# A row of maxima for the attention scores: TensorE products and a ScalarE copy replaced by a VectorE transpose and small DMAs

## The chip, the cores and the metric

The kernel runs on one core of a Trainium2 chip. The metric is the time of one execution on the device in microseconds (us). The engines are TensorE (PE, with its weight loads shown apart as PEld), VectorE (DVE), ScalarE (ACT), GpSimd (POOL) and SyncE (SP). Each works through its own list of instructions in order, and waits on semaphores where an operand comes from another engine or from a DMA. A DMA is issued by one of these lists, above all SP's, and lands some time later.

## The reference, cut to what matters

One encoder layer: a normalised input is projected once; eight mLSTM heads and eight attention heads work on the projection; an output projection and a gated feed-forward network follow. The change lies in the attention:

```python
q = rmsnorm(aq.reshape(B, T, A_KV_HEADS, G, HEAD_DIM), q_norm_w)
k = rmsnorm(ak.reshape(B, T, A_KV_HEADS, HEAD_DIM), k_norm_w)
...
s = jnp.einsum('bqhgd,bkhd->bhgqk', qi, k).astype(jnp.float32) * scale
p = jax.nn.softmax(s, axis=-1)
return jnp.einsum('bhgqk,bkhd->bqhgd', p.astype(v.dtype), v)
```

There are 8 query heads and 2 key/value heads of 64 dimensions, one sequence of 2048 tokens and one of 256. All is float32 at the interface.

## The kernel before, in words

The attention is cut into 36 blocks of one head (or of two, for the short sequence) by 512 queries: 32 blocks over 2048 keys and 4 over 256 keys. `attention` (a Python generator) writes the instructions of one block after another, one block ahead of itself:

- `prep` loads the queries of a block (`bq`, SP), transposes them on TensorE into the PSUM tile `pq` (L546) and copies them on ScalarE into two SBUF tiles: `qq` (L549), 128 partitions, the high part of each query in partitions 0 to 63 and the rest (low part) in 64 to 127; and `qm` (L551), the high part alone in partitions 0 to 63. Partition 64 of `qm` is left for the row of maxima. `qq` and `qm` each have two buffers.
- `maxstep` computes scores of 128 queries by 1024 keys in a PSUM tile `px` (L570, two products of 128x512; in the short blocks L564) and VectorE takes their maximum per query into `mx` (L572, L566). Here queries lie on partitions.
- `prep2` reduces the partial maxima to one per query, negated (`m4r`, 128 queries by 4 groups, L578). The scores proper need them the other way round, as a row over 512 queries. Before the change four TensorE products `pr` (L581), of `m4r` broadcast against an identity, do this, and ScalarE copies one partition of the result into partition 64 of `qm` (L583).
- `scores` computes transposed scores, 128 keys by 512 queries, twice per step, into a PSUM tile `ps`: L591 with `qq`, and L592 with `qm` against keys that have a row of ones as row 64, so that the negated maximum is added in the product. ScalarE takes the exponential (L595) and its rounded copy (L596), VectorE the remainder (L597).
- `values` multiplies with the values (L608 to L610), three steps behind the scores; `fin1` and `fin2` divide and store the result for the output projection (`mix_d`).

The PSUM tiles `pq`, `px`, `ps` and, before the change, `pr` share two buffers (tag "sc"). In the loop of a block the max steps of the next block are spread over the first six of its eight steps and `prep2` of the next block follows them.

Around the attention run, on the same engines, the mLSTM heads (their projections are L729, L739 and L757, with inputs `mn`, `mjn`, `mvn` loaded through SP at L726 and L754) and, when these are done, the output projection of phase C (L1009, with loads `cmx` and `cx`, stores `x_d` and `n_d`, all on SP). `run_both` interleaves the generators by fixed costs per step. The final order on each engine is made at build time by the scheduler, which orders the written instructions by priority on a simulated timeline. Removing or adding an instruction therefore moves thousands of others. After both comes the feed-forward network (L1177 and later), where the attention has no part.

Of the kernel before, what the change touches and what calls it, by code (L numbers as in the profile page):

```python
# [9 lines left out]
F32 = mybir.dt.float32  # L10
F32R = mybir.dt.float32r
AF = mybir.ActivationFunctionType
# [5 lines left out]
P = 128  # L18
# [6 lines left out]
HD = 64  # L25
# [60 lines left out]
def f32(ap):  # L86
    return ap.bitcast(F32)
# [380 lines left out]
def attention(g, tc, s1, s2, pp):  # L468


    nc = g.nc
    sp = s1
# [48 lines left out]
    def load_q(n):  # L521

        if n in qzs or n >= len(hbs):
            return
        t = 0
        qz = qzs[n] = sp.tile([P, 4, P], F32R, tag="qz", name=f"bq{n}", bufs=QZB)
        for h, q0, q1 in hbs[n][1]:
            nc.sync.dma_start(f32(qz[:, t:t + q1 - q0]), g.q_d[h, q0:q1].rearrange("n p d -> p n d"))
            t += q1 - q0

    def prep(n):

        s = HB()
        grp, s.qs, k0, k1 = hbs[n]
        s.n = n
        s.last = n == len(hbs) - 1
        load_q(n)
        load_kv(grp, k0, k1)
        s.kv = kv[(grp, k0)]
        s.nq, s.nk = 4, k1 - k0  # L540
        s.N = s.nq * P
        s.nm = "%d_%d" % s.qs[0][0:2]
        qz = qzs.pop(n)
        pq = pp.tile([P, 1024], F32R, tag="sc", name="pq" + s.nm)
        for t in range(s.nq):
            nc.tensor.transpose(pq[:, t * P:(t + 1) * P], qz[:, t, :], g.identr)  # L546
        load_q(n + 1)
        s.qq = sp.tile([P, 512], F32R, tag="qq", name="qq" + s.nm, bufs=2)
        nc.scalar.activation(s.qq[:, 0:s.N], f32(pq[:, 0:s.N]), AF.Copy)  # L549
        s.qm = sp.tile([65, 512], F32R, tag="qm", name="qm" + s.nm, bufs=2)  # L550
        nc.scalar.activation(s.qm[0:HD, 0:s.N], f32(pq[0:HD, 0:s.N]), AF.Copy)  # L551
        s.mx = sp.tile([P, 4, 2], F32, tag="mx", name="mx" + s.nm, bufs=2)
        s.nsp = -(-s.nk * P // 1024)
        s.todo = [(t, z) for z in range(s.nsp) for t in range(s.nq)] if s.nk * P > 512 else [(None, 0)]
        s.steps = len(s.todo)
        return s
# [17 lines left out]
    def prep2(s):  # L574

        nq = s.nq
        m4r = s.m4 = sp.tile([P, 4], F32R, tag="m4r", name="m4r" + s.nm, bufs=2)
        nc.vector.tensor_reduce(m4r[:, 0:nq], s.mx[:, 0:nq, 0:s.nsp], AX.X, ALU.max, negate=True)  # L578
        pr = pp.tile([P, 1024], F32, tag="sc", name="pr" + s.nm)
        for t in range(nq):  # L580
            nc.tensor.matmul(pr[:, t * P:(t + 1) * P], m4r[:, t:t + 1].to_broadcast([P, P]), g.identr, start=True,  # L581
                             stop=True)
        nc.scalar.activation(s.qm[HD:HD + 1, 0:s.N], pr[HD:HD + 1, 0:s.N], AF.Copy)  # L583

    def scores(s, kp):
        kk, kl1 = s.kv[kp // 2][0:2]
# [32 lines left out]
    def fin2(s):  # L619
# [10 lines left out]
        for h, q0, q1 in s.qs:  # L630
# [6 lines left out]
            if h == 5:  # L637
                g.mixed5.update(range(q0, q1))

    cur = prep(0)  # L640
    while cur.todo:
        maxstep(cur)
        yield 0.5
    prep2(cur)
    load_kv(0, 0, NT1, cur.m4)
    pend, fins = [], []
# [8 lines left out]
    for n in range(len(hbs)):  # L655
        nxt = prep(n + 1) if n + 1 < len(hbs) else None
        if n == len(hbs) // 2 - 1:
            load_kv(1, 0, NT1)
        nkp = cur.nk // 2
        for kp in range(nkp):  # L660
            pend.append((cur, *scores(cur, kp)))
            ready = bool(fins)
            if len(pend) > PLAG:
                drain()
            if nxt is not None and nxt.todo:
                for _ in range(-(-len(nxt.todo) // max(nkp - kp - MXE, 1))):
                    maxstep(nxt)
                if not nxt.todo:
                    prep2(nxt)
            if ready:  # L670
                fin2(fins.pop(0))
            yield 2.3
        if nxt is not None and nxt.todo:
            while nxt.todo:
                maxstep(nxt)
            prep2(nxt)
        cur = nxt
# [1002 lines left out]
```

## Time and profile before

| what | value |
|---|---|
| median of 3 runs | 3293.55 us (3292.37 to 3298.3) |
| profiled execution, time | 3297.57 us |
| profiled execution, span | 3295.9 us |
| TensorE busy | 3233.3 us (98%) |
| VectorE busy | 2427.5 us (74%) |
| ScalarE busy | 1959.4 us (59%) |
| mean granted TensorE clock | 0.993 |
| first and last product of the row of maxima (L581) | 217.7 us, 1713.2 us |

The profiled execution lies 4.0 us above the median and within the spread of the runs; 1.7 us of it lie outside the span. Busy times of PE come from matmuls whose ends are modelled and overlap; the distance from one start to the next is what a matmul holds the engine. In the views, "PEq", "SPq" and so on are the instruction lists themselves, with their semaphore and DMA-issuing instructions.

### The profile page before, as it was taken

The numbers are of one execution on the slowest core, as the hardware profiler recorded it, in microseconds if no ns is written. First come the engines' busy times: TensorE is split into PE (matmuls) and PEld (weight loads), VectorE is DVE, ScalarE is ACT, GpSimd is POOL, SyncE is SP. The second block draws the span as 40 slices with busy tenths as digits, with TensorE's granted clock in tenths as the row PEclk, the third lists the DMA queues.
The fourth block names the chain that finished last, engine by engine and source line by source line (L and its number), as shares of the span: only waits on it lengthen the run. The fifth ranks groups of instructions, "written<-read, shape, count | busy, mean of one in ns | idle before, by whom it ended". The sixth has DMA issues, their size and how long they took to land.

```text
span 3295.9 us, 52861 instructions
## 1 busy us (share of the span) xinstructions
PE 3233.3 (98%) x19488; PEld 3016.8 (92%) x19488; DVE 2427.5 (74%) x3683; ACT 1959.4 (59%) x3628; POOL 533.4 (16%) x922
## 2 busy tenths in 40 slices
PE   8999999999999999999999999999999999999998
PEld 7888888888888888878989999999999999999998
DVE  7754676677657777876666999988888788666664
ACT  5645666666665676654453555666676667454543
POOL 4561042213232333200000000000000000010201
PEclk9999999999999999999999999999999999999999
DMA  9973333343345444523327666768576567968663
GB/s 348 319 204 115 114 106 98 100 132 100 103 122 173 136 123 140 155 95 99 111 95 257 236 227 213 247 228 274 203 260 239 194 210 249 320 229 274 217 233 133
DMA packets 358857, 612.27 MB, mean 186 GB/s; under 512 B 31029, under 2 KB 215271, under 8 KB 358599
## 3 DMA queue, kind: packets, MB, share of 16 engines
q1 hardware_dynamic: 328855, 562.09, 50.6%
q0 software_dynamic: 12176, 35.01, 3.9%
q10 hardware_dynamic: 17568, 11.80, 1.1%
q8 instruction: 153, 2.51, 0.3%
q14 instruction: 105, 0.86, 0.1%
HBM read 444.85 MB, written 163.93 MB: 185 GB/s over the span
## 4 chain that ended last, share of the span: by engine, by line
PE 83%; DVE 4%; DMA 4%; issue 4%; ACT 3%; POOL 2%; SPq 1%; ACTq 0%; POOLq 0%; DVEq 0%
PE pa L1177 16%; PE pc L1177 8%; PE pf L1442 7%; PE po L1009 6%; PE pb L1177 4%; PE mj L729 4%; PE mv L739 4%; PE ph L1442 4%; PE pj L248 4%; PE ps L591 3%; PE ps L592 3%; PE pv L610 3%; PE pv L608 3%; PE pv L609 3%; PE px L570 3%
## 5 line engine op out<-in xcount | busy, mean ns | idle before, releaser
L597 DVE TENSOR_TENSOR xx<-pe,xx 128x1024 fp32r<-128x1024 f32 x260 | 318.1, 1224 | 147.7 <-ACT xx L596 145.5
L595 ACT ACTIVATE pe<-ps 128x1024 f32<-128x1024 f32 x260 | 266.2, 1024 | 240.0 <-PE ps L592 217.3
L572 DVE TENSOR_REDUCE mx<-px 128x1 f32<-128x1024 f32 x256 | 310.3, 1217 | 99.8 <-PE px L570 98.2
L596 ACT ACTIVATE xx<-pe 128x1024 fp32r<-128x1024 f32 x260 | 274.9, 1058 | 8.6 <-PE pv L610 3.4
L1395 POOL TENSOR_TENSOR sq<-sq,sq 128x384 f32<-128x384 f32 x38 | 48.4, 1274 | 1380.3 <-ACT sq L1391 1297.7
L1009 PEld LDWEIGHTS po<-cmx,wo 128*128 128x128 f32 x1728 | 228.0, 189 | 18.3 <-DVE cx L1016 1.4
L1009 PE MATMUL po<-cmx,wo 128*128 128x256 f32 x1728 | 235.8, 282 | 1.3 <-DVE cx L1016 1.3
L1182 ACT ACTIVATE u<-pa 128x386 f32<-128x386 f32 (+2 forms) x264 | 128.9, 489 | 169.0 <-PE pa L1177 168.1
L591 PE MATMUL ps<-qq,kk 128*128 128x512 f32 x520 | 213.9, 411 | 5.9 <-DVE mx L572 4.0
L610 PE MATMUL pv<-xx,vv 128*128 128x512 f32 x520 | 210.7, 405 | 3.5 <-DVE xx L597 3.5
L608 PE MATMUL pv<-xx,vv 128*128 128x512 f32 x520 | 209.9, 404 | 2.9 <-ACT xx L596 2.6
L592 PE MATMUL ps<-qm,kl 65*128 65x512 f32 x520 | 209.2, 402 | 0.0
L609 PE MATMUL pv<-xx,vl 128*64 128x512 f32 x520 | 206.8, 398 | 0.0
L729 PEld LDWEIGHTS mj<-mn,wm 128*128 128x128 f32 x1296 | 179.8, 194 | 18.4 <-ACT og L745 4.0
L729 PE MATMUL mj<-mn,wm 128*128 128x256 f32 x1296 | 190.1, 289 | 3.4 <-ACT og L745 3.1
L739 PE MATMUL mv<-wm,mn 128*128 128x256 f32 x1296 | 191.9, 286 | 1.3 <-ACT qb L735 1.3
L739 PEld LDWEIGHTS mv<-wm,mn 128*128 128x128 f32 x1296 | 177.4, 190 | 16.6 <-ACT qb L735 2.3
L248 PE MATMUL pj<-w_a,n1T 128*128 128x512 f32 (+1 forms) x864 | 168.2, 353 | 11.7 <-ACT w_a L105 7.0
L248 PEld LDWEIGHTS pj<-w_a,n1T 128*128 128x128 f32 x864 | 141.5, 192 | 31.5 <-ACT w_a L105 7.0
L570 PE MATMUL px<-kk,qq 128*128 128x512 f32 x512 | 166.3, 405 | 4.0 <-ACT pe L595 2.5
L840 ACT ACTIVATE dm<-dm,tm 128x128 f32<-128x128 f32 x288 | 95.0, 391 | 97.3 <-POOL dm L837 95.2
L1177 PE MATMUL pc<-nt,wb 128*128 128x386 f32 (+2 forms) x792 | 146.2, 338 | 1.3 <-DVE cx L1037 1.3
(332 smaller groups left out, 8073.7 us busy)
## 6 DMA issues: line engine op xcount, KB each, us to landing
mn<-n_d SPq DMA_DIRECT2D x216, 256.0 KB, 3.1
ru<-w_up SPq DMA_DIRECT2D x88, 512.0 KB, 5.0
rs<-wsu_d SPq DMA_DIRECT2D x88, 512.0 KB, 6.2
act_d<-ts SPq DMA_DIRECT2D x33, 768.0 KB, 6.1
nt<-act_d SPq DMA_DIRECT2D x60, 384.0 KB, 4.8
re_t<-wsd_d SPq DMA_DIRECT2D x45, 512.0 KB, 6.1
wsu_d<-tw SPq DMA_DIRECT2D x44, 512.0 KB, 4.5
act_d<-ya SPq DMA_DIRECT2D x99, 192.0 KB, 3.1
```

Of the source, the lines that this page charges most:

```text
L248: nc.tensor.matmul(pjs[t][:, c0:c1], nTs[tiles[t]][:, c, a, :], ws[c][:, b, c0:c1], start=(c == 0 and k == 0), stop=(c == NCC - 1 and k == 2))
L572: nc.vector.tensor_reduce(s.mx[:, t0, z0:z0 + 1], ps, AX.X, ALU.max)
L591: nc.tensor.matmul(o, kk[:, kc:kc + P], s.qq, start=True, stop=False)
L592: nc.tensor.matmul(o, kl1[:, kc:kc + P], s.qm, start=False, stop=True)
L597: nc.vector.tensor_tensor(x[:, 1], pe, f32(x[:, 0]), ALU.subtract)
L608: nc.tensor.matmul(s.pv, vv[:, kt % 4, :], x1, start=kt == 0, stop=False)
L610: nc.tensor.matmul(s.pv, vv[:, kt % 4, :], x2, start=False, stop=kt == s.nk - 1)
L729: nc.tensor.matmul(pj[:, o].rearrange("p (n t) -> p n t", t=P), s.w[c][:, a, o * P:(o + 1) * P], nT[c][:, :, h, :], start=(c + o + k == 0) ...
L739: nc.tensor.matmul(pv[:, o], nT[c][:, o, a, :], s.w[c][:, h, 256:512], start=(c + o + k == 0), stop=(c == NCC - 1 and k == 2 and o == 1))
L1009: nc.tensor.matmul(po[:, o], wo[c][z // 2][:, a, n], mx[c][:, h, :], start=c + o + k == 0, stop=c == NCC - 1 and o == 1 and k == 2)
L1177: m = s.nc.tensor.matmul(p, w[:, aa, c, :], ops[k][:, c, bb, 0:s.n], start=c == 0 and i == 0 and not add, stop=c == NCC // 2 - 1 and i == ...
L1442: nc.tensor.matmul(ps[c], w[:, aa, c, :], t[:, gi - g0, bb, 0:H], start=gi == 0 and m == 0 and not more, stop=gi == NG - 1 and m == 2, ski ...
```

## The change

The copy of the high query rows from PSUM by ScalarE becomes a DMA on SP from `qq` to `qm`, both in SBUF. The four products and ScalarE's copy of one row become: a VectorE transpose in blocks of 32x32, whose input is `m4r` with its four columns repeated eight times, so that within each block of 32 queries the maxima come to lie along a row; and four DMAs on SP that each take four partitions of 32 numbers and put them at the right places of partition 64 of `qm` (16 pieces of 128 bytes in all).

```diff
@@ prep
-        nc.scalar.activation(s.qm[0:HD, 0:s.N], f32(pq[0:HD, 0:s.N]), AF.Copy)
+        nc.sync.dma_start(f32(s.qm[0:HD]), f32(s.qq[0:HD]))
@@ prep2
         nc.vector.tensor_reduce(m4r[:, 0:nq], s.mx[:, 0:nq, 0:s.nsp], AX.X, ALU.max, negate=True)
-        pr = pp.tile([P, 1024], F32, tag="sc", name="pr" + s.nm)
-        for t in range(nq):
-            nc.tensor.matmul(pr[:, t * P:(t + 1) * P], m4r[:, t:t + 1].to_broadcast([P, P]), g.identr, start=True,
-                             stop=True)
-        nc.scalar.activation(s.qm[HD:HD + 1, 0:s.N], pr[HD:HD + 1, 0:s.N], AF.Copy)
+        mt = sp.tile([P, 32], F32, tag="mt4", name="mt" + s.nm, bufs=2)
+        nc.vector.transpose(mt.rearrange("p (r t) -> p r t", t=4), f32(m4r).unsqueeze(1).to_broadcast([P, 8, 4]))
+        for k in range(4):
+            nc.sync.dma_start(f32(s.qm[HD:HD + 1]).rearrange("o (t k i) -> o k t i", t=4, i=32)[:, k],
+                              mt[32 * k:32 * k + 4])
```

The scheduler then puts the instructions of every engine in another order from the first attention block on. First place: TensorE, a block in the middle of the first group (its names end in `_8` with `qq_8_6162`, `qm_8_6164`; the block before it has `_4`). Before, the row's products stand ahead of the scores of the old block's seventh step:

```order
L739 MATMUL mv_5_7097<-wm_6_4824,mn_5_6_7032 128x256 x4
L739 MATMUL mv_5_7097<-wm_7_4825,mn_5_7_7033 128x256 x6
L581 MATMUL pr_8_6547<-identr,m4r_8_6545 128x128 x4
L591 MATMUL ps_4_6_6553<-qq_4_5687,kk_16_12_2584 128x512
L592 MATMUL ps_4_6_6553<-qm_4_5689,kl_16_12_2585 128x512
```

In the changed program nothing of this stands there, and the first scores of the new block read as follows:

```order
L610 MATMUL pv_4_6425<-xx_4_6_6559,vv_16_12_2586 128x512
L591 MATMUL ps_8_0_6775<-qq_8_6162,kk_16_0_2536 128x512
L729 MATMUL mj_5_7042<-mn_5_1_7027,wm_1_4819 128x256 x3
L729 MATMUL mj_5_7042<-mn_5_2_7028,wm_2_4820 128x256
L570 MATMUL px_8_0_0_6791<-kk_16_0_2536,qq_8_6770 128x512
L570 MATMUL px_8_0_0_6791<-kk_16_4_2552,qq_8_6770 128x512
L854 MATMUL mS_15_7386<-qb_7_2397,mkT_7_2396 128x256
L592 MATMUL ps_8_0_6775<-qm_8_6164,kl_16_0_2537 128x512
```

The four products are gone; L591, which needs `qq` alone, now comes seven matmuls ahead of L592, which needs the row, with work of others between the two.

Second place: SP's list at the same block (- is before, + is the change). `mn` are loads of the mLSTM projection, `bq` the queries of the next block, `qm<-mt` the row, `qm<-qq` the high rows of the next block:

```order
 L726 DMA mn_5_4_7030<-n_d 128x512
-L528 DMA bq_6160<-q_d 128x4x128
 L726 DMA mn_5_5_7031<-n_d 128x512
 L726 DMA mn_5_6_7032<-n_d 128x512
 L726 DMA mn_5_7_7033<-n_d 128x512
+L582 DMA qm_8_6164<-mt_8_6547 1x4x32 x4
+L528 DMA bq_6768<-q_d 128x4x128
+L551 DMA qm_8_6772<-qq_8_6770 64x512
 L726 DMA mn_6_0_7408<-n_d 128x512
```

Five DMAs per block are added to SP, the row's four behind the loads of one projection and ahead of the next block's queries, of its high rows, and of the loads of the next projection.

Third place: TensorE where the mLSTM heads end (L893 is their last product) and phase C begins (L1009 is its first). Before:

```order
L893 MATMUL mT_8_16795<-ident,hh_17_16732 128x128
L591 MATMUL ps_8_7_16238<-qq_8_14758,kk_16_12_10418 128x512
L592 MATMUL ps_8_7_16238<-qm_8_14760,kl_16_12_10419 128x512
L591 MATMUL ps_8_7_16238<-qq_8_14758,kk_16_12_10418 128x512
L592 MATMUL ps_8_7_16238<-qm_8_14760,kl_16_12_10419 128x512
L1009 MATMUL po_0_17076<-cmx_0_17008,wo_0_16814 128x256 x3
```

In the changed program:

```order
L609 MATMUL pv_8_17111<-xx_8_5_17209,vl_16_8_10410 64x512
L591 MATMUL ps_8_7_17301<-qq_8_16376,kk_16_12_10418 128x512
L592 MATMUL ps_8_7_17301<-qm_8_16378,kl_16_12_10419 128x512
L591 MATMUL ps_8_7_17301<-qq_8_16376,kk_16_12_10418 128x512
L592 MATMUL ps_8_7_17301<-qm_8_16378,kl_16_12_10419 128x512
L1009 MATMUL po_0_17076<-cmx_0_17008,wo_0_16814 128x256 x3
```

The four `_8` blocks of the second group of heads have the queries `qq_8_14758`, `qq_8_15541`, `qq_8_16376` and `qq_8_16913`. Phase C began with the last scores of the first of them and begins now with the last scores of the third: the attention has moved ahead of the other work by two blocks. The mLSTM's last product stood four rows ahead of phase C and stands 17 rows ahead now, with attention alone between.

## The prediction

> **What bounds the kernel now.** I read the page first, then the busy times by stage, then what TensorE waited for in the stage of the attention.
>
> ```profile
> span 3295.9 us, 52861 instructions
> PE 3233.3 (98%) x19488; PEld 3016.8 (92%) x19488; DVE 2427.5 (74%) x3683; ACT 1959.4 (59%) x3628; POOL 533.4 (16%) x922
> PE 83%; DVE 4%; DMA 4%; issue 4%; ACT 3%; POOL 2%; SPq 1%; ACTq 0%; POOLq 0%; DVEq 0%
> ```
>
> TensorE is busy 98% of the span and holds 83% of the chain that ended last. The attention runs from about 200 to 1760 us. The view by stage (length, then busy us of PE, PEld, DVE, ACT, POOL; at the end granted clock, DMA share, GB/s) shows where it is not the bound:
>
> ```profile
> 200.00:300.00 100.00, 92.72 (x657) 83.79 (x656) 43.86 (x67) 49.62 (x118) 37.57 (x86) 0.98 0.59 166
> 300.00:1380.00 1080.00, 1067.01 (x6694) 933.19 (x6693) 756.31 (x1351) 696.93 (x1543) 300.92 (x589) 0.99 0.40 122
> 1380.00:1450.00 70.00, 60.73 (x298) 44.89 (x297) 58.24 (x103) 48.56 (x86) 6.99 (x12) 0.98 0.37 116
> 1450.00:1750.00 300.00, 300.00 (x1963) 267.38 (x1962) 195.83 (x281) 149.94 (x201) 15.86 (x21) 1.00 0.29 95
> ```
>
> TensorE is idle 7.3 us at the start, 13.0 us in the next 1080, 9.3 us in the 70 us in which the mLSTM heads end and attention is nearly alone (VectorE 83% busy there), and not at all after. So 1380 of these 1550 us are set by how much TensorE has to do. What it waited for, in total us, times and longest, is spread thin:
>
> ```profile
> PE ps L591 <- DVE mx L572: 4.0, 4, 1.7
> PE mj L729 <- ACT og L745: 3.1, 4, 1.0
> PE ps L591 <- ACT qm L583: 0.7, 1, 0.7
> PE mj L729 <- DMA mn<-n_d: 0.3, 1, 0.3
> ```
>
> The row of maxima itself, whose ScalarE copy is L583, cost TensorE 0.7 us of waiting, once. Its price must be looked for in the work.
>
> **The products that go.** Two of the 36 groups of four in the timeline, with what follows each (start, us, count at the end), and the group of all 144 by lines (after the bar: busy us, mean ns, idle before):
>
> ```profile
> 263.61 0.64 PE L581 MATMUL pr<-identr,m4r 128*128 128x128 f32 x4
> 264.08 0.50 PE L546 MATMUL pq<-identr,bq 128*128 128x128 f32 x4
> ...
> 1713.02 0.56 PE L581 MATMUL pr<-identr,m4r 128*128 128x128 f32 x4
> 1713.41 0.45 PE L591 MATMUL ps<-qq,kk 128*128 128x512 f32 x1
> 1713.70 0.39 PE L592 MATMUL ps<-qm,kl 65*128 65x512 f32 x1
> 1713.93 0.40 PE L591 MATMUL ps<-qq,kk 128*128 128x512 f32 x1
> ...
> 1754.73 11.23 PE L1009 MATMUL po<-cmx,wo 128*128 128x256 f32 x93
> ...
> L581 PE MATMUL pr<-identr,m4r 128*128 128x128 f32 x144 | 21.9, 271 | 0.1
> ```
>
> The mean of 271 ns times 144 would be 39 us, but these matmuls overlap. From its start to the next start a group holds TensorE 0.39 us (1713.02 to 1713.41) or 0.47 us (263.61 to 264.08): 36 of them are 14.0 to 16.9 us. The 21.9 us of the group count each tail that overlaps with the next matmul, and are an upper bound. I take 0.43 x 36 = **-15.5 us**.
>
> **ScalarE's copies.** They are 36 x (0.580 + 0.589) = 42 us less, and 43.8 us in which ScalarE stood in its order waiting for the products:
>
> ```profile
> L551 ACT ACTIVATE qm<-pq x36: 575/580/594, 208.7 to 1670.4; 64x512 fp32r<-64x512 f32 x36
> L583 ACT ACTIVATE qm<-pr x36: 572/589/593, 218.6 to 1713.6; 1x512 fp32r<-1x512 f32 x36
> ACT qm L583 <- PE pr L581: 43.8, 20, 5.8
> ```
>
> ScalarE is 65% busy from 300 to 1380 us (696.93 of 1080), so this is no time by itself. It and a PSUM buffer that is now passed on sooner can shorten TensorE's waits on ScalarE and on `mx` (3.1 and 4.0 us in the rows above): 0 to -7 us, taken as **-1**, since these waits have other causes as well.
>
> **More waits on TensorE.** The first L592 of a block waited for one ScalarE semaphore or none, and now for four or five of DMAs. In the order 23 groups of L581 wait for two semaphores, and the trace has 23 instructions on that line that only wait: each semaphore beyond the first costs one.
>
> ```profile
> L581 PEldq EVENT_SEMAPHORE  x23: 51/51/51, 263.0 to 1710.7; - x23
> ```
>
> Counting the waits in both orders, extra ones rise from 452 to 510: 58 x 0.051 = **+3.0 us** if none is covered, 0 if all are.
>
> **The new way of the row.** Reduction, transpose, four issues, landing, and only then L592. VectorE's part, the nearest transposes (64x512), and when the reduction L578 began after the last max product had been given to TensorE, in an early and in the last block:
>
> ```profile
> L578 DVE TENSOR_REDUCE m4r<-mx x36: 143/154/163, 214.7 to 1709.8; 128x4 fp32r<-128x8 f32 x32, 128x4 fp32r<-128x4 f32 x4
> L626 DVE STREAM_TRANSPOSE rs<-rc x36: 698/707/708, 282.9 to 1751.2; 64x512 f32<-64x512 f32 x36
> ...
> 382.48 0.63 PE L570 MATMUL px<-kk,qq 128*128 128x512 f32 x2
> 384.41 0.16 DVE L578 TENSOR_REDUCE m4r<-mx 128x4 fp32r<-128x8 f32 x1
> ...
> 1703.95 0.63 PE L570 MATMUL px<-kk,qq 128*128 128x512 f32 x2
> 1709.79 0.15 DVE L578 TENSOR_REDUCE m4r<-mx 128x4 fp32r<-128x8 f32 x1
> ```
>
> From the end of the products (start plus 0.63) to the reduction are 1.3 and 5.2 us, which are also the least and the most of the 36; the median is 2.3. The transpose has 32 columns instead of 512, so it lies between nothing and 0.7 us; I take 0.15, as for the reduction, which is as small. VectorE gets 36 x 0.15 = 5 us more in 1550, most of it where it waits for others. For issue and landing of SP's DMAs (the list's own time, then from issue to landing; the first pair is `mn`, 128 partitions, the second `mix_d`, the third line has 17 partitions):
>
> ```profile
> L726 SPq DMA_DIRECT2D mn<-n_d x216: 319/320/1403, 167.6 to 979.2; - x108
> DMA to landing us min/median/max: 2.7/3.1/13.0
> L899 SPq DMA_DIRECT2D mix_d<-mmx x9: 319/320/382, 1294.5 to 1423.3; - x9
> DMA to landing us min/median/max: 1.9/2.2/3.4
> L465 SPq DMA_DIRECT2D nm_d<-nst x5: 239/239/791, 214.7 to 235.0; - x5
> ```
>
> Four issues are 4 x 0.239 = 0.96 to 4 x 0.320 = 1.28 us; landing lies between 1.9 and 3.1 us, 2.5 taken for 512 bytes that no row matches. Median chain: 2.3 + 0.15 + 0.15 + 1.1 + 2.5 = 6.2 us; before it was the products and a ScalarE copy, about 1.2 us behind their place. Against it stands the work that the order puts between the last max product and the first L592. For the block of the first place that is 23 matmuls of 512 columns, 30 of 256 and 11 short ones; at 0.23 (1713.70 to 1713.93), 0.12 (11.23/93) and 0.11 us (0.43/4) 10.1 us. Over the 36 blocks it is 6.7 to 13.9 us, median 9.2, and once 30. So the row is about 3 us early at the median. Late reductions (up to 2.9 us over the median) against short covers (2.5 us under it) make a few blocks late: at a landing of 2.5 us some 0.05 us a block on average, at 3.1 us about 0.1. I take **+2 us** for all, 0 to +35 as bounds, the upper one with the rivals.
>
> The Trainium skill (DMA: Bandwidth & Descriptors, "Anatomy of one DMA") gives a fixed cost of about 2.0 us per DMA, most of it the receipt of the write. The trace's shortest 1.9 us agrees. By it the median chain would be 5.7 us and this term +1, an estimate.
>
> SP's list gets 180 DMAs. Behind the row's four stand the next queries, the next high rows and the next projection's `mn`. If the row is late in being given to SP, `mn` is late next. In the order the first `mn` behind the row has 8 us or more of TensorE's work between its buffer coming free and its first use, against 3.1 us of landing; ahead of the row `mn` loads wait for matmuls that end at most 2.9 us after the last max product, before the transpose is due by the median. So I cost the queue at nothing; the high rows (needed some 45 us of work later) too. In phase C the row stands behind stores `x_d` that wait for results of TensorE and VectorE, with 10 to 14 us of cover.
>
> **The order around it.** The attention moves ahead by two blocks (third place). Summing the order at the paces above, the stretch between the last mLSTM projections and an even mixture with phase C holds 39 us of attention in 50 before, 50 in 60 now. Stretch 1380 to 1450 lost 9.3 us for its 39; at the same rate 50 lose 12: **+2.5 us**, between -9 (the new order mends it) and +9 (it is lost twice).
>
> Sum: -15.5 - 1 + 3 + 2 + 2.5 = -9. The profiled execution's 3297.57 would become 3288.5; the median of the runs, 4.0 us lower, 3293.55 becomes **3284.5 us**. This case's own range is -2.5 to -18 us, 3275.5 to 3291.
>
> **The rivals.** *The row comes late (slower).* Place: the first L592 of each block. With a landing of 5.8 us, the longest of `bq`,
>
> ```profile
> DMA to landing us min/median/max: 2.6/3.3/5.8
> ```
>
> which other loads on the queue could cause, the chain is 9.5 us against 9.2; with the spread of both, the mean wait of a block is near 1 us, 35 us in all: -11 + 35 = +24, about 3317 us. It decides from a mean wait of 0.3 us a block (11/36). For it: the scheduler already put L591 and L592 apart, so in its own reckoning the row comes no sooner; and waits cost twice, as the clock shows:
>
> ```profile
> 1005.00:1010.00 5.00, 2.66 (x16) 1.92 (x15) 3.62 (x6) 0.86 (x2) 0.00 (x0) 1.00 0.88 286
> 1010.00:1015.00 5.00, 3.97 (x21) 3.35 (x21) 4.36 (x10) 1.78 (x3) 0.00 (x0) 0.74 0.53 189
> 1015.00:1020.00 5.00, 5.00 (x25) 4.61 (x24) 1.87 (x6) 3.01 (x5) 0.00 (x0) 0.58 0.66 208
> ```
>
> After 3.4 idle us in ten the granted clock is 0.74 and then 0.58, which takes 0.26 x 5 + 0.42 x 5 = 3.4 us more. The Trainium skill (TensorE: Matmul & The Clock Gate, "Part 1: The HAM clock gate") names an idle window of about 3.4 us for the drop to half speed; the trace has the drop with no single gap of that length, so shorter waits are not safe either. Against this rival: the DMA share is 0.29 to 0.40 from 300 us on, and the small `mix_d` land in 2.2 us.
>
> *The work is given back (no change).* The new order loses more where attention is alone, or at the start, where TensorE idles 7.3 us and queries, keys and rows share a DMA system that is 0.59 busy. With the +9 of the alone stretch instead of +2.5 the sum is -2.5: about 3291 us.
>
> *More than the work (faster still).* The freed ScalarE and PSUM buffer remove half of the 29.6 us of TensorE's idling: -9 - 15 = -24, 3269.5 us. For it: 43.8 us of ScalarE's blocked order go. Against: TensorE's rows of waits on ScalarE are small.
>
> **How the numbers follow.** Forecast 0.48, given back 0.22, late 0.20, more 0.10. 0.2% is 6.6 us, about what a measurement of this kernel can tell from no change. The forecast's own range has a quarter of its chance above -6.6. Faster: 0.36 + 0.10 + a little of the second case = 0.50; same: 0.12 + 0.16 = 0.28; slower: 0.20 + 0.02 = 0.22. The range for 8 in 10 leaves out half of the late case and a part of the best: 3268 to 3308 us.
>
> **What would show it.** Right: L581, L551 and L583 on TensorE and ScalarE are gone; rows of `qm` land within 2.5 us or so; L592 has no DMA among what ended its idle time, or a few us in all; TensorE's idling from 200 to 1760 us stays near 30 us, and phase C ends some 10 us sooner. Wrong: "PE ps L592 <- DMA qm" with more than 11 us; a granted clock under 1.00 at block boundaries; `mn` with more than its 0.3 us as a releaser; or a longer stretch with VectorE over 83% busy around 1400 us.

## The result, and the profile after

The changed kernel takes 3276.49 us (median of 6 runs, 3268.71 to 3278.38) against 3293.77 us for the kernel before in the same runs: 0.9934 of it, interval 0.9921 to 0.9948. That is faster by 17.3 us by the medians and by 22 (17 to 26) by the ratio, where the forecast was 9 us. (The ratio stands for a kernel before of about 3297 us, as in the later groups of runs below; the mean of the six runs beside the change is 3294.2 us.) The profiled execution of the change is its fastest one (3268.71 us, 7.8 below its median), and that of before lay 4.0 above its own, so the two traces differ by 28.9 us, more than the kernels do. 5.5 of these lie ahead of the first attention block (its first `pq` is at 202.1 instead of 207.6 us). A difference of a few us between the traces proves nothing, and the sizes below are checked by runs.

The page of the change:

```profile
span 3266.9 us, 52932 instructions
PE 3207.5 (98%) x19344; PEld 2992.7 (92%) x19344; DVE 2437.6 (75%) x3719; ACT 1920.7 (59%) x3556; POOL 538.4 (16%) x922
PE 85%; DMA 4%; issue 3%; DVE 3%; ACT 3%; POOL 2%; SPq 1%; ACTq 0%; POOLq 0%; DVEq 0%
```

144 matmuls fewer, TensorE as full as before. The stages in the same bounds (length, then busy us of PE, PEld, DVE, ACT, POOL; at the end granted clock, DMA share, GB/s):

```profile
200.00:300.00 100.00, 90.51 (x622) 80.53 (x622) 43.36 (x67) 44.28 (x107) 37.42 (x86) 0.97 0.54 156
300.00:1380.00 1080.00, 1073.84 (x6700) 936.15 (x6699) 790.02 (x1390) 690.54 (x1508) 298.03 (x586) 1.00 0.40 125
1380.00:1450.00 70.00, 64.65 (x337) 49.35 (x335) 62.93 (x112) 48.61 (x90) 14.15 (x20) 1.00 0.39 119
1450.00:1750.00 300.00, 294.58 (x2042) 267.99 (x2043) 198.77 (x319) 133.44 (x191) 12.91 (x18) 1.00 0.44 143
```

TensorE idles more at the start (9.5 us instead of 7.3) and after 1450 us (5.4 instead of 0), and less between: 6.2 us instead of 13.0 from 300 to 1380, 5.4 instead of 9.3 in the 70 us after it. The attention itself ends earlier, by far more than its work shrank: the last `pv` starts at 1675.3 us instead of 1749.1, and phase C then runs longer alone. What TensorE waited for from 200 to 1760 us (total us, times, longest):

```profile
PE mj L729 <- DMA mn<-n_d: 4.9, 3, 4.1
PE po L1009 <- DVE cx L1016: 3.9, 2, 2.6
PE pv L610 <- DVE xx L597: 2.6, 6, 0.8
...
PE ps L591 <- DVE mx L572: 1.4, 3, 0.9
...
PE ps L592 <- DMA qm<-mt: 1.0, 1, 1.0
```

The row of maxima was late once in 36 blocks, by 1.0 us. New at the head is `mn`, the load of the mLSTM projection, with 0.3 us before. The instructions that the change adds (count, then shortest, median and longest ns):

```profile
L580 DVE STREAM_TRANSPOSE mt<-m4r x36: 178/211/214, 209.7 to 1614.4; 128x32 f32<-128x32 f32 x36
L582 SPq DMA_DIRECT2D qm<-mt x144: 572/577/699, 210.6 to 1617.0; - x144
L551 SPq DMA_DIRECT2D qm<-qq x36: 502/534/1546, 203.6 to 1570.0; - x36
L592 PEldq EVENT_SEMAPHORE  x73: 51/51/199, 214.4 to 1619.3; - x73
L570 PEldq EVENT_SEMAPHORE  x10: 51/51/1126, 220.1 to 957.4; - x10
```

One of the row's four DMAs holds SP's list for 0.577 us, and one of the high rows for 0.534, where the larger DMAs in the prediction's rows took 0.239 to 0.320.

**Where the time went.** For each trace I took TensorE's matmuls in order of time, from the first `pq` to the end of the last `po`, and split each distance from one start to the next into the idle time that the trace puts ahead of the second one and the rest, which the first one held. This stage is 1595.6 us before and 1570.3 after. The loss of clock is half of the time in which the trace has the clock at half speed and TensorE is not idle.

| part of the stage | before | after | change |
|---|---|---|---|
| products `pr` (L581), start to start | 15.5 | 0 | -15.5 |
| time lost to the granted clock | 8.4 | 1.6 | -6.8 |
| other work of TensorE | 1543.0 | 1543.2 | +0.2 |
| idle: waits for `mx` and for the exponential `pe` | 9.1 | 4.8 | -4.3 |
| idle: waits for `mn` | 0.3 | 4.9 | +4.6 |
| idle: wait for the row | 0.0 | 1.0 | +1.0 |
| idle: all others | 19.3 | 14.7 | -4.6 |

This is one trace of each kernel. Which of these rows belong to the change, and which to this one execution and order, is told by the traces of the experiments below.

### The profile page after: what moved, and what is told of

Its sections match the earlier page's. It is cut to its first block, busy times and chain, and to the rows that moved or that the text cites. A ratio compares the mean times of both kernels' runs of the same rounds, so it can differ in the third digit from the quotient of the medians.

```text
span 3266.9 us, 52932 instructions
## 1 busy us (share of the span) xinstructions
PE 3207.5 (98%) x19344; PEld 2992.7 (92%) x19344; DVE 2437.6 (75%) x3719; ACT 1920.7 (59%) x3556; POOL 538.4 (16%) x922
## 4 chain that ended last, share of the span: by engine, by line
PE 85%; DMA 4%; issue 3%; DVE 3%; ACT 3%; POOL 2%; SPq 1%; ACTq 0%; POOLq 0%; DVEq 0%
PE pa L1177 17%; PE pc L1177 9%; PE pf L1442 7%; PE po L1009 5%; PE ph L1442 4%; PE pb L1177 4%; PE mv L739 4%; PE mj L729 4%; PE pv L610 3%; PE ps L591 3%; PE ps L592 3%; PE pv L608 3%; PE pv L609 3%; PE px L570 3%; PE pj L248 2%
## 5 line engine op out<-in xcount | busy, mean ns | idle before, releaser
L597 DVE TENSOR_TENSOR xx<-pe,xx 128x1024 fp32r<-128x1024 f32 x260 | 319.3, 1229 | 142.4 <-ACT xx L596 139.6
L595 ACT ACTIVATE pe<-ps 128x1024 f32<-128x1024 f32 x260 | 265.2, 1022 | 229.1 <-PE ps L592 204.6
L1009 PEld LDWEIGHTS po<-cmx,wo 128*128 128x128 f32 x1728 | 221.2, 189 | 16.1 <-DVE cx L1016 4.2
L1009 PE MATMUL po<-cmx,wo 128*128 128x256 f32 x1728 | 227.7, 281 | 3.9 <-DVE cx L1016 3.9
L591 PE MATMUL ps<-qq,kk 128*128 128x512 f32 x520 | 211.3, 406 | 3.6 <-DVE mx L572 1.4
L592 PE MATMUL ps<-qm,kl 65*128 65x512 f32 x520 | 208.2, 401 | 1.0 <-DMA qm<-mt 1.0
L729 PEld LDWEIGHTS mj<-mn,wm 128*128 128x128 f32 x1296 | 180.4, 192 | 26.0 <-DMA mn<-n_d 5.8
L729 PE MATMUL mj<-mn,wm 128*128 128x256 f32 x1296 | 192.2, 287 | 7.8 <-DMA mn<-n_d 4.9
L570 PE MATMUL px<-kk,qq 128*128 128x512 f32 x512 | 166.6, 407 | 2.3 <-ACT pe L595 1.6
```

What stands on the lines that cost most here:

```text
L591: nc.tensor.matmul(o, kk[:, kc:kc + P], s.qq, start=True, stop=False)
L592: nc.tensor.matmul(o, kl1[:, kc:kc + P], s.qm, start=False, stop=True)
L597: nc.vector.tensor_tensor(x[:, 1], pe, f32(x[:, 0]), ALU.subtract)
L729: nc.tensor.matmul(pj[:, o].rearrange("p (n t) -> p n t", t=P), s.w[c][:, a, o * P:(o + 1) * P], nT[c][:, :, h, :], start=(c + o + k == 0) ...
L1009: nc.tensor.matmul(po[:, o], wo[c][z // 2][:, a, n], mx[c][:, h, :], start=c + o + k == 0, stop=c == NCC - 1 and o == 1 and k == 2)
```

## The experiments

The theory after the result: the gain is the products' 15.5 us and a few more, because their place was dear too (the first half held, the second did not show in the kernel's own gain, as the traces under "The order alone" tell). A product `pr` takes one of two PSUM buffers (tag "sc") through which every `pq`, `px` and `ps` must pass, and holds it until the maxima are there. The rivals: the relief of ScalarE (two copies less a block); the order that the scheduler happened to choose; SP's list. Where a product, a transpose or a DMA is added, its result is read by nobody and nothing of the computation is left out, unless a line says otherwise. The ratio is to the kernel before, run beside each group (medians 3293.77 us for the change, then 3297.17 for e1, e2, e3 and e6, 3298.31 for e8, e9, e4 and e5, 3297.82 for e11, e10 and e7, 3299.71 for e12). The last column is (ratio - 1) x 3297 us, and the text goes by it, since the medians of the kernel before differ between the groups. In kernels with two added lines the later line numbers are higher by two (in e3 by four): L593, L594 and L597 of e5 are L591, L592 and L595 elsewhere.

| kernel | edit | median, us | ratio [95%] | against before, us |
|---|---|---|---|---|
| the change | | 3276.49 | 0.9934 [0.9921, 0.9948] | -21.8 |
| e1_row_only | change, high rows by ScalarE | 3278.47 | 0.9936 [0.992, 0.9951] | -21.1 |
| e2_high_only | before, high rows by DMA | 3306.20 | 1.0029 [1.0018, 1.004] | +9.6 |
| e3_products_back | change + four products | 3313.03 | 1.0045 [1.0032, 1.0058] | +14.8 |
| e6_before_transpose | before + transpose | 3299.63 | 1.0005 [0.9997, 1.0013] | +1.6 |
| e8_extra_products | change + four transposes on TensorE, no buffer of their own | 3298.27 | 1.0003 [0.9992, 1.0014] | +1.0 |
| e9_slot_only | change + one small product of the maxima in an "sc" buffer | 3309.39 | 1.0037 [1.0024, 1.0049] | +12.2 |
| e4_rows_on_pool | change, row issued by GpSimd | 3277.30 | 0.9942 [0.9927, 0.9956] | -19.1 |
| e5_late_row | change + one DMA more ahead of the row | 3288.48 | 0.9968 [0.9957, 0.998] | -10.6 |
| e11_slot_no_wait | e9 with a ready operand | 3294.31 | 0.9989 [0.9977, 1.0] | -3.6 |
| e10_rows_pool_high_act | e1 and e4 together | 3284.83 | 0.9957 [0.9942, 0.9971] | -14.2 |
| e7_rows_on_act_queue | change, row issued by ScalarE | 3283.67 | 0.9952 [0.9935, 0.9969] | -15.8 |
| e12_second_transpose | change + second transpose | 3275.04 | 0.9927 [0.9913, 0.994] | -24.1 |

### One half of the change alone

e1 has the row by DMA and ScalarE's copy of the high rows:

```diff
-        nc.sync.dma_start(f32(s.qm[0:HD]), f32(s.qq[0:HD]))
+        nc.scalar.activation(s.qm[0:HD, 0:s.N], f32(pq[0:HD, 0:s.N]), AF.Copy)
```

> The changed kernel with the high rows of qm copied by ScalarE from PSUM again (36 x 0.58 us); the row of maxima still goes by transpose and four DMAs. TensorE does exactly the work of the changed kernel. If TensorE's work sets the time: within 3 us of the changed kernel, 15 to 19 us under before. If ScalarE's relief is half of the gain: some 5 us over the changed kernel, since 21 of the 42 us of copies come back, while the copy that stood blocked behind the products stays away. If SP's list costs something: up to 5 us under the changed kernel, since 36 DMAs leave it.

e2 is the kernel before with the reverse of this edit.

> The kernel before with the high rows copied by the DMA; products and ScalarE's row copy stay. If TensorE's work sets the time: as before, within 3 us. If ScalarE's relief counts: 3 to 6 us under before. If the added DMAs on SP hold up other loads: a few us over before.

With the row alone the ratio is that of the change within 0.0002, as the first expectation had it: the row carries the whole gain, and nothing shows for the 36 x 0.58 = 21 us of ScalarE's copies. The high rows alone lose 9.6 us. Their DMA held up no matmul in e2. What grew are waits for ScalarE's exponential (TensorE's waits from 200 to 1760 us):

```profile
PE ps L591 <- ACT pe L595: 6.2, 7, 1.5
PE pv L608 <- ACT o L617: 3.8, 2, 2.0
PE px L570 <- ACT pe L595: 3.3, 4, 1.7
```

All waits for `pe` together are 9.5 us against 3.8 before. In the whole stage TensorE idles 34.9 us instead of 28.7 and loses 11.8 us to the clock instead of 8.4, which together are as much as the 9.6 us. Why these waits grow when ScalarE has less to do these runs don't say; e1 has 7.2 us of them and is no slower than the change.

### The order alone

The scheduler moves thousands of instructions for any edit. e6 adds the new transpose to the kernel before, and e12 a second one to the change:

```diff
+        mt = sp.tile([P, 32], F32, tag="mt4", name="mt" + s.nm, bufs=2)
+        nc.vector.transpose(mt.rearrange("p (r t) -> p r t", t=4), f32(m4r).unsqueeze(1).to_broadcast([P, 8, 4]))
```

> The kernel before with the VectorE transpose added, whose result nobody reads (36 x 0.21 us on VectorE, nothing on the path of the row). It is a control for the scheduler's order. If the order makes no difference by itself: within 3 us of before. If any rearrangement moves the time by its own stalls: 5 us or more to either side.

> The changed kernel plus a second transpose of the maxima per block into a tile that nobody reads: 36 times 0.2 us on VectorE, nothing on TensorE, no PSUM buffer, no wait. It measures what the scheduler's new order alone does to the changed kernel. Five such orders without further TensorE work came to 3276.5, 3278.5, 3277.3, 3283.7 and 3284.8 us. Theory (the order alone scatters by a few us, so that the forecast of about 3284 us and the measured 3276.5 us are one mechanism in two orders): 3276 to 3287 us. Rival (the gain beyond the 15.5 us of products hangs on the one order that the changed kernel happens to have): 3288 to 3300 us, as the kernels with a further product reached.

+1.6 us on the one side and, against the change's own -21.8, -2.3 on the other; at 3275.04 us e12 is just under what the theory gave it, and far from the rival. Six kernels have the row by DMA, no product added and no further delay (the change, e1, e4, e7, e10, e12). They stand at -14.2 to -24.1 us against before, mean -19.4. So the gain doesn't hang on one lucky order, and a difference of 5 us between two such kernels isn't read as an effect.

The traces of the six, split as above, say what the gain is made of. Their profiled executions lie 19.3 us under that of before on average, as the runs do:

| part of the stage | before | the change | mean of the six | least and most of the six |
|---|---|---|---|---|
| products `pr` | 15.5 | 0 | 0 | 0 |
| time lost to the granted clock | 8.4 | 1.6 | 6.2 | 1.6 to 11.5 |
| other work of TensorE | 1543.0 | 1543.2 | 1542.7 | 1539.1 to 1545.1 |
| all idle time | 28.7 | 25.4 | 28.3 | 25.4 to 31.3 |
| whole stage | 1595.6 | 1570.3 | 1577.2 | 1570.3 to 1585.8 |

Of 18.4 us on average 15.5 are the products. The trace of the change has the least idle time and the least loss of clock of the six, so what its own table shows of these beyond the products is mostly this execution and this order. What all six have in common is a shift: idle time rises in the first 40 us of the stage (3.6 us before, 6.1 to 7.9 in the six), falls where the attention is nearly alone, 1170 to 1250 us into the stage (9.2, now 3.6 to 5.5), and rises behind that (1.3, now 3.4 to 5.2).

### The products' work without their place

e8 adds four more TensorE transposes a block, into the half of `pq` that is unused: work as of the old products, but no buffer of their own and no wait for the maxima.

```diff
         for t in range(s.nq):
             nc.tensor.transpose(pq[:, t * P:(t + 1) * P], qz[:, t, :], g.identr)
+        for t in range(s.nq):
+            nc.tensor.transpose(pq[:, (4 + t) * P:(5 + t) * P], qz[:, t, :], g.identr)
```

> The changed kernel with four more transposes per block, written into the unread half of the query tile pq at the start of a block: as many 128-column matmuls as the row's products, but no further PSUM buffer and no wait for the maxima. The first run with the products put back stood 1.1% over the changed kernel, twice their own 15.5 us. If TensorE's work alone is it: 12 to 17 us over the changed kernel, ratio to before about 0.998. If the place of the products (their PSUM buffer and their wait for the maxima) makes the other half: also 12 to 17 us here, and the rest shows in the run with the buffer alone. If any added matmul costs double: 30 us and more over the changed kernel.

Start to start, `pq` holds TensorE 23.7 us instead of 11.2 in the change: 12.5 us of work. The time is 20 us above the mean of the six and 22 above the change, between what the expectations had (12 to 17 and 30 or more). The 8 us beyond the work are more than any of the six lies from their mean (4.7 us below to 5.2 above it) and less than the 9.9 us between the two farthest, so they aren't read as an effect. In the profiled execution, e8's fastest, the stage is 16.2 us above the mean of the six traces: 12.5 of work, 3.2 more of idle time and no more loss of clock (6.0 us). So in that trace the work put back is paid once.

### The place without the work

e9 adds one product of 4 columns a block, which takes an "sc" buffer and needs the maxima; e11 takes the buffer with an operand that is ready. (The two last lines are one line of each kernel.)

```diff
+        pr = pp.tile([P, 1024], F32, tag="sc", name="pr" + s.nm)
+        nc.tensor.matmul(pr[:, 0:4], g.ident, f32(m4r), start=True, stop=True)     # e9
+        nc.tensor.matmul(pr[:, 0:4], g.ident, g.ident[:, 0:4], start=True, stop=True)   # e11, in its place
```

> The changed kernel with one small product of four columns per block that takes one of the two shared PSUM buffers after the maxima, as the row's products did; its work is some 4 us in all. If TensorE's work alone is the gain: 0 to 6 us over the changed kernel. If the PSUM buffer and the wait for the maxima cost as much as the work: 12 to 22 us over it.

> The changed kernel plus one product of 4 columns per block (identity against four of its own columns; nobody reads it) that takes one of the two shared PSUM buffers, written at the place of the former products but waiting for no maxima. The same product with the maxima as operand came to 3309.4 us, 1.0037 of before, with about 5 us of product work. Theory A (a further taker in the rotation of two shared PSUM buffers costs, whatever it waits for): again about 3309 us, between 3303 and 3315. Rival B (only the wait for the maxima costs, since a buffer stands claimed until they are there): near the changed kernel, 3277 to 3286 us. Between 3286 and 3303 both have a part.

The small products hold TensorE 5.4 us in e9 and 6.0 in e11, start to start. e9 is 32 us above the mean of the six, 26 beyond its work, and 33 above the change by the medians, more than either expectation had. e11 is 16 above the mean, 10 beyond its work, and its 3294.31 us lie between the two expectations, where both have a part. So a product that takes a buffer and waits for the maxima costs several times its work here, and the wait seems the larger part of it: 16 us lie between two kernels that differ in the operand of one product, more than lies between any two of the six. Whether the turn of the buffer costs anything by itself is not settled; 10 us is like the 8 of e8, which took no buffer. In e9's trace TensorE idles 41.8 us in the stage, 16.4 more than in the change, and 13.8 of these lie from 900 to 1380 us. The window in the kernel before, the change, e11 and e9:

```profile
900.00:1380.00 480.00, 469.16 (x2899) 406.91 (x2899) 347.60 (x656) 310.49 (x709) 153.76 (x294) 0.99 0.46 143
```

```profile
900.00:1380.00 480.00, 474.98 (x2972) 412.65 (x2971) 362.86 (x676) 309.74 (x710) 156.85 (x304) 1.00 0.48 149
```

```profile
900.00:1380.00 480.00, 469.05 (x2885) 405.36 (x2883) 354.30 (x649) 302.46 (x676) 147.71 (x286) 0.99 0.48 140
```

```profile
900.00:1380.00 480.00, 461.20 (x2818) 394.46 (x2817) 340.57 (x638) 292.70 (x660) 141.64 (x280) 0.99 0.48 140
```

TensorE idles 10.8, 5.0, 11.0 and 18.8 us in these 480 us. No single wait stands behind e9's number. In its waits, the largest are 5.4 us for `mn` and 3.7 for `mx`, and many others are of 1 to 3.4 us. Against the mean of the six traces it idles 13.5 us more and loses 6.8 more to the clock; some 6 us of its 31.9 are in neither of these nor in the product.

### Everything back, with the DMAs kept

e3 puts the four products into the change, unread; the row still comes by DMA.

```diff
+        pr = pp.tile([P, 1024], F32, tag="sc", name="pr" + s.nm)
+        for t in range(nq):
+            nc.tensor.matmul(pr[:, t * P:(t + 1) * P], m4r[:, t:t + 1].to_broadcast([P, P]), g.identr, start=True,
+                             stop=True)
```

> The changed kernel with the 144 products of the row put back into a PSUM tile that nobody reads: their work and their PSUM buffer come back, the ScalarE copies do not, and the row still goes by DMA. If TensorE's work is the gain: 13 to 18 us over the changed kernel, at the time of before to 4 us under it. If ScalarE's relief is the larger part: no more than 5 us over the changed kernel.

34 us above the mean of the six and 37 above the change by the medians, more than twice what either expectation had. In the traces its stage is 34.0 us above the mean of the six: the products hold 16.1 start to start, the clock takes 13 more (19.1 against 6.2) and TensorE idles 5.4 more. It is also 14.8 us above the kernel before, which has the same products. So the place of the products has not one price. In the kernel before it came to little, since all of its difference from the six is 19.4 us and 15.5 are work; beside the new DMAs it is 18 (e3) to 26 (e9). What makes it dear there is open.

### The lists that issue the row

e4 and e10 let GpSimd issue the row's DMAs (e10 with the high rows on ScalarE, so that SP's list is as before), e7 lets ScalarE.

```diff
-            nc.sync.dma_start(f32(s.qm[HD:HD + 1]).rearrange("o (t k i) -> o k t i", t=4, i=32)[:, k],
+            nc.gpsimd.dma_start(f32(s.qm[HD:HD + 1]).rearrange("o (t k i) -> o k t i", t=4, i=32)[:, k],
```

> The changed kernel with the row's four DMAs issued from GpSimd's list instead of SP's. In the changed kernel they hold SP 133 us waiting for the transpose, and late mn loads cost TensorE 4.9 us near 225 us. If SP's order is what is left to gain: 3 to 8 us under the changed kernel, no mn among TensorE's waits. If GpSimd's own waits (mix_d, dm) make the row late: TensorE waits for qm at the first L592 of blocks, 5 us or more over the changed kernel.

> The changed kernel with the row's four DMAs issued by GpSimd and the high rows copied by ScalarE again, so that SP's list is as before the change. Theory (SP's extra 180 issues cost 2 to 5 us through late mn loads at the start, and no more): 3272 to 3279 us, mn at most 1 us among TensorE's waits. Rival (the issues cost nothing at all where they stand, and ScalarE's 21 us of copies and GpSimd's dearer issue take as much): 3279 to 3285 us.

> The changed kernel with the row's four DMAs issued from ScalarE's list, which then stands about 2.5 us per block in issuing (90 us in all) and waits for each transpose. Theory (ScalarE's own order is not what sets the end, at 64 per cent busy): 3276 to 3285 us. Rival (ScalarE standing still for the maxima was a good part of what the change removed; exponentials come late, PSUM buffers are held): 3295 to 3315 us, with more of TensorE's idling put down to ScalarE and to px, ps buffers.

No list is better than SP beyond the scatter. e4, at 3277.30 us, met neither case: it is not under the change, and TensorE waited 0.8 us for the row. e7 is where the theory had it; e10, at 3284.83 us, is at the far end of what its rival had, in which SP's issues cost nothing that moving them would win (GpSimd's issue wasn't dearer, 0.514 us against 0.577, and ScalarE's copies can't be told from the scatter). Off SP, `mn` still held TensorE for 2.1 us in e4 and 3.3 in e10. Issuing the row's 144 DMAs holds ScalarE 144 x 0.580 = 84 us in e7, and other ScalarE work waits behind it, without the end moving by more than an order does. ScalarE in e7, the last rows saying who waited for that line (us, times):

```profile
L582 ACTq DMA_DIRECT2D qm<-mt x144: 580/580/1182, 214.6 to 1644.7; - x144
...
  ACT xx L596: 11.9, 7
  ACT pe L595: 10.3, 5
```

That is a second sign, beside e1, that ScalarE's time doesn't set the end here.

### How early the row is

e5 copies the transposed block into another tile by a DMA first, so the row is one issue and one landing later.

```diff
+        mu = sp.tile([P, 32], F32, tag="mu4", name="mu" + s.nm, bufs=1)
+        nc.sync.dma_start(mu, mt)
```

> The changed kernel with one more DMA hop between the transpose and the row's four DMAs (SBUF to SBUF, all 128 partitions): the row is some 2.5 us later in every block. In the changed kernel the row was ready about 1.5 us before its first use at the median and TensorE waited 1.0 us for it in all. The scheduler knows of the hop and may set the first use later. If the row's lateness is near to deciding: TensorE waits for qm in half of the blocks, 10 to 35 us over the changed kernel. If the scheduler finds other work for the time: within 5 us of the changed kernel.

9 us more than the mean of the six, 11 more than the change. The time is in the range of the first case, but not by its mechanism alone. TensorE's waits in e5:

```profile
PE ps L593 <- ACT pe L597: 5.1, 7, 1.7
PE ps L594 <- DMA qm<-mu: 4.6, 5, 1.8
```

5 blocks of 36 and not half of them wait for the row, by 1.8 us at most and 4.6 us in all. TensorE idles 36.1 us in this stage, where the six have 28.3 on average; the rest of the difference is spread over other waits and the clock. The cover is real and has an end: a hop more and it is used up in some blocks.

## Why the prediction was right, and where it was off

**TensorE's work sets the time.** Right. The part that the forecast was built on, -15.5 us for the products, holds: the trace of before has 15.5 us for them start to start, e3 16.1, and e8 shows that work put back is paid (12.5 us of work, 20 us of time by the runs, 16 in its trace). The six traces have nothing but the products as a gain that is clear of their scatter.

**The row's way.** Right within its bounds, though its terms were too small and only the cover made up for it. The transpose took 0.211 us instead of 0.15. The four issues take 4 x 0.577 = 2.3 us instead of 1.1, because the rows they were priced from, loads of 17 and 128 partitions, were not like them. The landing was taken as 2.5 us. The trace of the change has no landings for these DMAs, but e4's has, where GpSimd issues them:

```profile
DMA to landing us min/median/max: 1.5/2.3/6.8
```

So the choice was good, and with 2.3 us the median chain is 2.3 + 0.15 + 0.21 + 2.3 + 2.3 = 7.3 us instead of 6.2; the cover of 9.2 us still holds it. The 2.0 us that the prediction had from the Trainium skill (DMA: Bandwidth & Descriptors, "Anatomy of one DMA") stand there for DMAs that GpSimd issues; e4's median is near that figure, and its shortest landing is under it. Where TensorE did wait in the change, the last issue began at 214.72 + 1.82 - 0.6 = 215.9 us, and the L592 that waited started at 220.07, so there the landing was some 4.1 us. The charge of +2 us became 1.0 (0.6 to 2.3 in the six, or 4.4 in e7 with the wait that is named below). The rival "The row comes late" had its place right and its price wrong; e5 shows it beginning.

**The queue at nothing.** Wrong. At the start of the attention `mn` was late, as the prediction's list of wrong signs had it. SP's list and TensorE there (start, us, engine, line, count; in brackets idle time and what ended it), with lines of others left out:

```profile
214.72 1.82 SPq L582 DMA_DIRECT2D qm<-mt  x3
...
217.49 1.16 SPq L726 DMA_DIRECT2D mn<-n_d  x2
...
218.85 0.59 SPq L551 DMA_DIRECT2D qm<-qq  x1
219.48 0.58 SPq L726 DMA_DIRECT2D mn<-n_d  x1
...
220.07 0.47 PE L592 MATMUL ps<-qm,kl 65*128 65x512 f32 x1 [0.98 <-DMA qm<-mt]
...
221.41 4.66 SPq L726 DMA_DIRECT2D mn<-n_d  x3
225.53 1.65 PE L729 MATMUL mj<-mn,wm 128*128 128x256 f32 x6 [4.08 <-DMA mn<-n_d]
```

The row and the high rows stand between the loads of `mn`, and the last three of these then need 4.66 us to be given at all, one of them 3.7 us:

```profile
L726 SPq DMA_DIRECT2D mn<-n_d x216: 319/320/3713, 164.0 to 984.7; - x108
```

The prediction had counted cover from the time at which the buffer of `mn` is free, and not from the time at which the load is given. The clock falls with the gap:

```profile
220.00:225.00 5.00, 1.39 (x6) 0.87 (x6) 1.77 (x2) 3.20 (x4) 3.05 (x10) 0.70 1.03 271
225.00:230.00 5.00, 4.47 (x21) 3.92 (x22) 0.68 (x1) 0.38 (x1) 1.15 (x3) 0.62 1.04 278
```

The gap reaches from 221.45 to 225.53 us, so the clock's loss in the first window falls into idle time and costs nothing more. 4.08 us of waiting and at most 0.38 x 5 = 1.9 us of clock are some 6 us in all. The wait comes with the row's DMAs, not with those of the high rows: of the eleven kernels with the row by DMA ten wait 2.1 to 7.0 us for `mn` at L729, and the kernel before, e2 and e6 0.3 at most. (The eleventh is e7. Its trace puts a wait of 2.7 us down to `mn`, but at an L592, which doesn't read `mn`; that wait was likely for the row.) With the row on GpSimd's list 2.1 (e4) and 3.3 us (e10) are left, and these kernels are no faster. The DMA share is over 1.0 at this place, but it is so in the kernel before and in e2 too, without such a wait:

```profile
225.00:230.00 5.00, 5.00 (x41) 4.67 (x40) 1.23 (x1) 2.65 (x5) 1.57 (x4) 1.00 1.05 241
```

```profile
225.00:230.00 5.00, 5.00 (x33) 4.37 (x33) 0.00 (x0) 0.03 (x1) 3.38 (x12) 1.00 1.08 298
```

So full DMA engines alone don't make the wait. What their part is, no run tells.

**What was mis-sized: the charges +3, +2 and +2.5.** The work came off and these came on only in part.

- *Extra semaphore waits, +3.* The two orders were counted to 58 more. In the traces, the instructions of TensorE that only wait, summed over all lines of the stage, rise from 314 to 330: L592 has 73, but L581 lost its 23 and L570 fell from 34 to 10. 16 x 0.051 = 0.8 us, if none is covered.
- *The attention-alone stretch, +2.5.* Its idle time fell from 9.3 to 5.4 us, so -3.9, inside the bounds of -9 to +9 and on their other side. Idle time came up later instead (5.4 us after 1450), so this is a shift as much as a gain. All six kernels have it. One sign of being wrong that the prediction named for this place, VectorE over 83% busy, came true (62.93 of 70 us, 90%), and TensorE idled less there and not more.
- *ScalarE and the PSUM buffer, -1.* Waits for `mx` and `pe` fell by 4.3 us in the pair of traces, and from 9.1 to 7.3 us in the mean of the six (4.8 to 10.6). The range of 0 to -7 holds both. No run shows a part of ScalarE in it (e1, e7); a buffer that is held for the maxima can be dear (e9 against e11). How much of the kernel's own gain is due to it can be bounded only: 19.4 us in the mean of the six less 15.5 of work leaves 4 us, with the scatter of the order as large, and all idle time fell by 0.4 us in that mean.

So the forecast of 3284.5 us was 8 us too slow in its likeliest value, and 3276.5 lies at the fast end of its own range (3275.5 to 3291). That range is a choice: the bounds of the terms add up to far more than -18 to -2.5. It charged 7.5 us for troubles that came to 0.8 + 1.0 - 3.9 = -2.1 us by the pair of traces, or +3.3 with the idle time behind the stretch, and charged nothing for `mn`, which came to 4.6. That these errors partly cancel is luck. It left out the clock, which gave 6.8 us in the pair of traces; in the six it is 1.6 to 11.5 us against 8.4, so this is no steady part of the gain, and the mean of the six medians (3279.3 us) is nearer to the forecast than the change itself.

**What would show it.** The row's wait is of 1.0 us (right). Idle time from 200 to 1760 us stays near 30 (right: 29.5 before and 26.4 after, to 1750). Phase C was to end some 10 us sooner; it ends 30.8 us sooner in the traces (1803.2 to 1772.4 us), 5.5 of them from ahead of the stage, in two executions that lie farther apart than the kernels. Of its signs of being wrong, `mn` as a releaser came true. "The work is given back" didn't happen. "More than the work" had 3269.5 us, and the measured 3276.5 is about as near to that as to the forecast; but it named half of the idle time, and 3.3 of 28.7 us went (0.4 in the mean of the six). So it is the mechanism and not the number that tells the two apart.

## What to carry to other kernels

Where TensorE is full, count the removed matmuls from start to start and take that as the likeliest gain: here six kernels that lost 15.5 us of products are 14.2 to 24.1 us faster. A charge for a wait should be made only where its cover, worked out from the order, is short, and the cover of a load counts from when its list gives it, not from when its buffer is free. A helper product that takes a turn in a PSUM rotation and waits for another engine can cost several times its own 0.4 us through what passes through the rotation behind it, and its price changes with the order. Before a few us between two versions are explained, run one or two edits that change nothing but the order: here kernels that differ in little but the order lie up to 10 us apart.

## What the runs showed of the hardware

**An issue's time doesn't go by the bytes.** A DMA of 4 partitions of 128 bytes held its list 0.577 us on SP, 0.580 on ScalarE, and 0.514 on GpSimd (e4):

```profile
L582 POOL DMA_DIRECT2D qm<-mt x144: 502/514/622, 215.4 to 1630.0; - x144
```

The loads of `mn`, of 256 KB, took 0.320 in the prediction's row. Here four tiny DMAs hold an issuing list longer than four large ones.

**The clock falls in steps and after short gaps.** In all these traces the clock of the stage goes to half speed for 3.41 us or a multiple of it, mostly 3.41 or 6.83, so that a fall costs 1.7 or 3.4 us. In e3 two short gaps were enough for a step of 3.4. Its windows, and TensorE's waits in them:

```profile
1335.00:1340.00 5.00, 3.38 (x15) 2.75 (x15) 2.12 (x6) 4.33 (x9) 2.09 (x5) 0.81 0.29 83
1340.00:1345.00 5.00, 5.00 (x20) 4.43 (x19) 2.47 (x6) 3.08 (x6) 1.16 (x3) 0.51 0.45 124
```

```profile
1335.36 0.50 PE L614 MATMUL pv<-xx,vv 128*128 128x512 f32 x1 [0.49 <-DVE xx L601]
...
1337.81 1.67 PE L875 MATMUL mN<-va,dm 128*128 128x65 f32 x8 [1.26 <-POOL mr L98]
```

1.6 idle us in the first five, in gaps of 0.49 and 1.26, and (0.19 + 0.49) x 5 = 3.4 us of clock behind it. The Trainium skill (TensorE: Matmul & The Clock Gate, "Part 1: The HAM clock gate") has half speed begin after an idle window of about 3.4 us. A step of 1.7 us is one such window at half speed, which agrees; that it needs a gap of 3.4 us does not: here gaps of 0.49 and 1.26 us did, and 1.6 us of waiting cost 5 us in all. In e3 the clock took 19 us of the stage, more than all its products.

The 14 traces together bound what makes the clock fall. In this stage it fell to half speed 52 times. I summed TensorE's idle gaps (over 0.15 us each) in the 3.41 us ahead of every fall, and in all other pieces of 3.41 us at full speed, cut in step with the falls. Ahead of the falls they are 1.2 to 3.4 us, in one gap or several, and in 49 of the 52 no single gap filled the piece. In none of the pieces without a fall are they over 1.64 us. So in this kernel the idle share of such a piece, from about 0.35 to 0.5 of it upward, goes with the fall, and not the length of one gap.
